# A hybrid decoder layer: v of the first two token tiles from raw x in fp32, and seven of eight products with the norm gain on GpSimd

## The chip, the cores and the metric

The kernel runs on one core of one Trainium2 chip, in one launch. A core has a matrix engine (TensorE, PE in the profile), a vector engine (VectorE, DVE), a scalar engine (ScalarE, ACT), a general engine (GpSimd, POOL) and a sync engine (SyncE, SP) that here only issues DMAs. Each engine takes its instructions in the order of the program, and semaphores order them against each other. SBUF is the on-chip memory of 128 partitions, PSUM the memory that TensorE writes its products to.

The metric is the time of one execution on the device, in microseconds; of several runs the median is given.

## The reference

One layer, 1024 tokens of 1024 channels. Only its head matters here: the RMS norm with its gain, and the projection of the normed input, of which v is 512 columns.

```python
def rms_norm(x, g):
    xf = x.astype(jnp.float32)
    var = jnp.mean(xf * xf, axis=-1, keepdims=True)
    return (xf * lax.rsqrt(var + RMS_EPS) * g.astype(jnp.float32)).astype(x.dtype)

for l in range(DEPTH):                                   # DEPTH = 1
    h = rms_norm(x, norm_mix_pre[l])
    proj = h @ w_in[l]
    q, k, v, cb, cc, cx, g_att, g_conv = jnp.split(proj, IN_SPLITS, axis=-1)
    ...
```

After it come a causal stick-breaking attention over 8 heads of 64, a short gated convolution, their merge with sigmoid gates, an output projection with a norm and a residual, and a feed-forward part with a convolution of its own.

## The kernel before

**Precision.** Most products are made of fp16 halves: an operand is scaled by a power of two and split into a high half (its value in fp16) and a low half (what is left, again in fp16). A product then takes three fp16 passes (`PASSES`: high by high, high by low, low by high). The scale of a weight comes from the sum of its squares: ScalarE squares it with an accumulating output, `total` sums that over the partitions with a tiny matmul against ones and takes a power of two (`pow2_of`). The scale of the normed input, `s_h`, comes from the greatest gain (`g_top`, `g_max`). Where fp32 operands are multiplied without a split, TensorE takes them as fp32.

**Tiles and layouts.** x is cut into eight tiles of 128 tokens, `xt[0]` to `xt[7]`. TensorE needs the normed input with the channels on the partitions. That is `hT`, 128 partitions by 2 halves by 8 blocks of channels by 1024 tokens. A token tile gets there in one of three ways:

- Tile 0: normed in two halves of 512 channels (`norm_halves`, L263), turned by eight TensorE transposes (`turn_halves`, L283) and copied by ScalarE to `h32`, in fp32 (L502). Its v is made by `v_raw` (L353) from `h32` and the raw fp32 `w_v`: eight fp32 products. Its halves of hT are made from `h32` late (L543, L544).
- Tiles 1 and 2: normed, turned by `turn_pe` (L292), and split from PSUM straight into hT (L516, L517 and L526, L527). Their v takes three fp16 passes over eight blocks of channels (`v_pass`, L362).
- Tiles 3 to 7: normed by `norm` (L253), split in SBUF into `x16` (L304 on ScalarE, L305 on VectorE) and turned by two DMA transposes each, issued by SyncE (L308).

**The norm.** The sum of squares is made by ScalarE, or half by ScalarE and half by VectorE in `norm_halves`; GpSimd raises it to the power -1/2 (one number per token); VectorE multiplies x by that number and by the gain in one operation (L259, L275). For tiles 0 and 1 the gain is in PSUM: TensorE spreads the one loaded row of it over 128 partitions by two products with a row of ones (L249). For the others it is `gb`, a tile that a DMA fills with the row repeated.

**v.** `v_end` (L376) takes a tile's v out of PSUM with a scale (L381), makes differences of neighbouring tokens with the help of three small DMAs (L385), and splits them. The scale is 2^-16, or `vs0` for tile 0.

**Order.** SyncE's first loads are written by hand: x0, the first quarter of w_v, x1, the other three quarters, x2, the gain tile `gb`, x3, two tables and x4 to x7. Everything else is put in order by a planner (`Plan`). Each job has an engine, a cost and its reads and writes; `LAND` says when each x tile lands. TensorE jobs keep the order in which they are listed (`seq`), apart from a few, and the planner lists the others by the time at which they can start and by how late they may be. `warm(n)` is n products of a constant tile that nothing reads. After v of tiles 0 to 3 come the first halves of q and k of the first pair of heads (`qk_fill`, L467, products on L459), which read hT of tiles 0 to 3; then v of tile 4 and the second halves of q and k, which read hT of tiles 4 to 7; then the attention units with the other projections between them.

**Buffers.** The slab pool `s` has 12 slots of 4 KB per partition for this part, `wh` has eight buffers for split weights, `pm` three PSUM banks.

Of the kernel before, what the change touches and what calls it, by code (L numbers as in the profile page):

```python
# [18 lines left out]
F32 = mybir.dt.float32  # L19
# [5 lines left out]
P = 128  # L25
# [19 lines left out]
ONE = 2.0 ** 14  # L45


class Layer:
# [84 lines left out]
    def mixer(self, mid):  # L133
        tc, nc, a = self.tc, self.nc, self.a
        hT = self.hp.tile([P, 2, KD, T], F16, tag="hT", name="hT")
        with ExitStack() as ph1:
# [14 lines left out]
            if True:  # L151
# [5 lines left out]
                on1 = self.slot([P, P], F32, "on1")  # L157
# [28 lines left out]
                with tc.manual_schedule(engines={ET.PE, ET.DVE, ET.Activation, ET.SP, ET.Pool}):  # L186
# [28 lines left out]
                    LAND = {0: 4.6, 1: 7.3, 2: 12.9, 3: 15.9, 4: 18.6, 5: 20.0, 6: 21.4, 7: 22.8}  # L215
                    g_row, zero, one_row = given("s", gr, 2.3), given("s", wz), given("s", on1)
                    gbb = given("s", gb, 14.4)
                    xs = {tt: given("s", xt[tt], LAND[tt]) for tt in range(8)}
                    raw_v = [given("ws", st[i], (6.1, 8.7, 10.0, 11.5)[i]) for i in range(4)]
                    sv = given("sm", self.small("sm_v"))  # L220
                    hb = [NOTE() for _ in range(8)]
                    h32 = Buf("s", lambda: self.slot([P, KD, P], F32, "h32"))
# [23 lines left out]
                    gpb = Buf("z", lambda: two_banks("g_ps"))  # L246
                    ps2 = Buf("pm", lambda: pm.tile([P, NH], F32, tag="pm", name="g2"))
                    for c in range(2):
                        M(0.94, lambda c=c: pe.matmul(gpb.t.rearrange("p k t -> p (k t)")[:, ds(c * NH, NH)], on1[0:1, :],  # L249
                                                      gr[0:1, ds(c * NH, NH)], start=True, stop=True), [one_row, g_row], [(gpb, str(c))])  # L250
                    M(0.3, lambda: pe.matmul(ps2.t[:, 0:2], self.ones[0:1, :], g_c.t["g16"][0:1], start=True, stop=True),
                      [g_c], [ps2])
                    def norm(tt):  # L253
                        r, x = Buf("sm", lambda: self.small(f"r_pre{tt}")), xs[tt]
                        A(1.25, lambda: self.sumsq(xt[tt], r.t[:, 0:1], f"n_pre{tt}"), [x], [r])
                        V(0.15, lambda: vec.tensor_scalar(r.t[:, 1:2], r.t[:, 0:1], 1.0 / D, EPS, ALU.mult, ALU.add), [], [r])
                        pl.add("G", 0.6, lambda: pool.tensor_tensor(r.t[:, 2:3], r.t[:, 1:2], self.neghalf, ALU.pow), [], [r])
                        g = gpb if tt < 2 else gbb
                        V(1.28, lambda: vec.scalar_tensor_tensor(  # L259
                            xt[tt], xt[tt], r.t[:, 2:3], g.t.rearrange("p k t -> p (k t)") if tt < 2 else gb,  # L260
                            ALU.mult, ALU.mult), [r, g], [x])

                    def norm_halves(tt, first=(), prior=(), then=None):  # L263
                        r, x = Buf("sm", lambda: self.small(f"r_pre{tt}")), xs[tt]
                        lo, hi = xt[tt][:, :NH], xt[tt][:, NH:]
                        A(0.82, lambda: act.activation(self.junk(f"jk_n_pre{tt}")[:, :NH], lo, AF.Square, accum_out=r.t[:, 0:1]),
                          [(x, "0"), *first], [(r, "0")])
                        V(0.76, lambda: vec.scalar_tensor_tensor(jv.t[:, :NH], hi, 1.0, hi, ALU.mult, ALU.mult,
                                                                 accum_out=r.t[:, 3:4]), [(x, "1"), *prior], [(r, "1"), jv])
                        V(0.15, lambda: vec.tensor_scalar(r.t[:, 4:5], r.t[:, 3:4], 1.0 / D, EPS, ALU.mult, ALU.add), [], [(r, "1")])  # L270
                        V(0.15, lambda: vec.scalar_tensor_tensor(r.t[:, 1:2], r.t[:, 0:1], 1.0 / D, r.t[:, 4:5], ALU.mult, ALU.add),
                          [(r, "0"), (r, "1")], [(r, "2")])
                        pl.add("G", 0.6, lambda: pool.tensor_tensor(r.t[:, 2:3], r.t[:, 1:2], self.neghalf, ALU.pow), [], [(r, "2")])
                        for c, sl in enumerate((slice(0, NH), slice(NH, D))):
                            V(0.66, lambda sl=sl: vec.scalar_tensor_tensor(  # L275
                                xt[tt][:, sl], xt[tt][:, sl], r.t[:, 2:3], gpb.t.rearrange("p k t -> p (k t)")[:, sl],
                                ALU.mult, ALU.mult), [(r, "2"), (gpb, str(c))], [(x, str(c))])
                            if then and c == 0:
                                then(x)
# [3 lines left out]
                    def turn_halves(tt):  # L283
                        pt[tt] = [Buf("pm", lambda: pm.tile([P, KH, P], F32, tag="pm", name=f"pt_pre{tt}a")),
                                  Buf("z", lambda: two_banks(f"pt_pre{tt}b"))]
                        for c in range(2):
                            def f(c=c):
                                for k in range(KH):
                                    pe.transpose(pt[tt][c].t[:, k, :], xt[tt][:, ds((c * KH + k) * P, P)], self.ident)
                            M(0.52, f, [(xs[tt], str(c))], [pt[tt][c]])  # L290
# [11 lines left out]
                    def turn_dma(tt, due=1e9):  # L302
                        b, x = Buf("s", lambda: self.slot([P, 2, D], F16, f"x16_{tt}")), xs[tt]
                        A(1.06, lambda: act.activation(b.t[:, 0, :], xt[tt], AF.Copy, scale=s_h), [x, g_s], [(b, "0")], due=due)  # L304
                        V(1.27, lambda: vec.scalar_tensor_tensor(b.t[:, 1, :], xt[tt], s_h, b.t[:, 0, :], ALU.mult, ALU.subtract),  # L305
                          [x, g_s, (b, "0")], [(b, "1")], due=due)
# [40 lines left out]
                    own = hT[:, :, :, :P]  # L347
# [5 lines left out]
                    def v_raw(*ks):  # L353
                        def f():
                            for k in ks:
                                pe.matmul(pv[0].t, h32.t[:, k, :], st[k // 2][:, ds((k % 2) * NH, NH)], start=k == 0,
                                          stop=k == KD - 1)
                        M(0.87 * len(ks), f, [(h32, str(k // KH)) for k in ks] + [raw_v[k // 2] for k in ks], [pv[0]])
# [13 lines left out]
                    vs0 = Buf("sm", lambda: self.small("vs0"))  # L372

                    vf = {}

                    def v_end(tt):  # L376
                        f = vf[tt] = Buf("s", lambda: self.slot([P, 2, NH], F32, f"vf{tt}"))
                        v, b = v16[tt // 2], vb[tt // 2]
                        pj = lambda e: f.t[:, e].rearrange("p (j two d) -> p j two d", two=2, d=64)
                        sc = lambda: vs0.t[:, 0:1] if tt == 0 else 2.0 ** -16  # L380
                        A(0.58, lambda: act.activation(f.t[:, 0], pv[tt].t, AF.Copy, scale=sc()), [pv[tt]] + ([vs0] if tt == 0 else []),  # L381
# [118 lines left out]
                    square_v(0, 0, slice(0, D), "A")  # L500
                    for c in range(2):
                        A(0.55, lambda c=c: act.activation(h32.t[:, ds(c * KH, KH)], pt[0][c].t[:, :KH], AF.Copy, scale=s_h),  # L502
                          [pt[0][c], g_s], [(h32, str(c))])
                    square_v(1, 1, slice(0, D), "A", [h32])
                    square_v(2, 2, h0, "A")
                    square_v(2, 3, h1, "V", [xs[1]])
                    square_v(3, 4, h0, "A")
                    square_v(3, 5, h1, "V")
                    bv = total("v", sv, lambda: sv.t, 6, True, far=False)
                    V(0.15, lambda: vec.tensor_scalar(vs0.t[:, 0:1], bv.t["s"], 2.0 ** -16, None, ALU.mult), [bv], [vs0])  # L510
                    for k in range(3):
                        v_raw(k)
                    turn_pe(1)
                    for k in range(3, KD):
                        v_raw(k)
                    A(1.1, lambda: act.activation(hT[:, 0, :, ds(P, P)], pt[1].t, AF.Copy, scale=s_h), [pt[1], g_s], [(hb[1], "0")])  # L516
                    V(1.27, lambda: vec.scalar_tensor_tensor(hT[:, 1, :, ds(P, P)], pt[1].t, s_h, hT[:, 0, :, ds(P, P)],  # L517
                                                             ALU.mult, ALU.subtract), [pt[1], g_s, (hb[1], "0")], [(hb[1], "1")])
# [10 lines left out]
                    v_bank(1)  # L529
                    for i in range(4):  # L530
                        v_pass(1, (2 * i, 2 * i + 1), ((0, 0), (1, 0)), first=i == 0)
                    v_bank(2)
                    v_pass(2, range(4), ((0, 0),), first=True)
                    v_pass(2, range(4, 8), ((0, 0),))
                    v_pass(2, range(8), ((1, 0),))
                    for i in range(4):
                        v_pass(1, (2 * i, 2 * i + 1), ((0, 1),), last=i == 3)
# [1468 lines left out]
```

## Time and profile before

| | us |
|---|---|
| three runs: median (lowest to highest) | 1250.1 (1249.38 to 1251.72) |
| the profiled execution, its time on the device | 1250.39 |
| its span, first to last instruction | 1248.7 |

| engine | busy, us | share of the span |
|---|---|---|
| ACT | 856.1 | 69% |
| POOL | 86.3 | 7% |

The other engines' rows stand in the prediction. PE is matrix products; PEld, the loads of the stationary operand, runs beside them. "Busy" for PE contains products whose end is modelled, because they overlap in the array; the step from one start to the next is the better measure of what one costs. A row of the timeline has the start from the beginning of the span, the length, the engine, the line of the kernel, the operation with the tiles that it writes and reads, and in brackets how long the engine was idle before it and what ended that. A row of the waits names who waited, for whom, and the total, the number and the longest of the waits.

### The profile page before, as it was taken

To read this page: it belongs to the slowest core of one execution; us is meant where nothing else is said; L and a number is where in the kernel's file an instruction comes from. 1 tells how busy PE (TensorE), PEld (TensorE's weight loads), DVE (VectorE), ACT (ScalarE), POOL (GpSimd) and SP (SyncE) were. 2 spreads that over 40 slices of the span, in tenths; PEclk is the share of its full clock that TensorE was granted. 3 is DMA by queue.
4 is the path that set the end of the run, shared out by engine and by line. 5 is a ranking of instruction groups with operands and counts; after the bars stand their busy time and mean duration, and the time that the engine had idled before them with its cause. 6 is when DMAs were issued, how large, how long until landed. Compare 5 with 4: busy or idle time off the path is not lost.

```text
span 1248.7 us, 16478 instructions
## 1 busy us (share of the span) xinstructions
PE 1233.2 (99%) x6065; PEld 559.4 (45%) x6065; DVE 1018.6 (82%) x1605; ACT 856.1 (69%) x1247; POOL 86.3 (7%) x113
## 2 busy tenths in 40 slices
PE   9999999999999999999989999999999999999997
PEld 4444444444444444444444444444444444444443
DVE  7888889856998675559899999699589879969866
ACT  7766666736758565755666679778778967878434
POOL 1100000000000000001100001001100300111003
PEclk9999999999999999999999999999999999999999
DMA  8755577660224111656953205415921961594607
GB/s 276 157 128 116 136 129 180 148 150 29 74 74 129 34 65 54 233 189 149 222 144 133 71 23 214 169 34 99 257 82 19 203 184 34 104 251 142 179 1 135
DMA packets 148931, 160.80 MB, mean 129 GB/s; under 512 B 114425, under 2 KB 114553, under 8 KB 148850
## 3 DMA queue, kind: packets, MB, share of 16 engines
q1 hardware_dynamic: 138480, 123.05, 35.3%
q0 software_dynamic: 10368, 36.70, 14.1%
q8 instruction: 47, 0.77, 0.3%
q14 instruction: 34, 0.28, 0.1%
q10 hardware_dynamic: 2, 0.00, 0.0%
HBM read 92.88 MB, written 37.75 MB: 105 GB/s over the span
## 4 chain that ended last, share of the span: by engine, by line
PE 45%; DVE 2%; DMA 2%; issue 1%; ACT 1%; POOL 1%; POOLq 0%; DVEq 0%; SPq 0%; ACTq 0%
PE pq L1601 12%; PE pd L1671 2%; PE pu6b L1425 1%; PE pu10b L1425 1%; PE pu8b L1425 1%; PE pu20b L1425 1%; PE pu19b L1425 1%; PE pu16b L1425 1%; PE pu12b L1425 1%; PE pu4b L1425 1%; PE pu3b L1425 1%; PE pu21b L1425 1%; PE pu18b L1425 1%; PE pu17b L1425 1%; PE pu15b L1425 1%
## 5 line engine op out<-in xcount | busy, mean ns | idle before, releaser
L1425 PEld LDWEIGHTS <-wh_u 128*128 128x128 f16 x1848 | 179.1, 98 | 219.0 <-issue 2.2
L824 ACT ACTIVATE wh_u<-ws_u,sc_u 128x1024 f16<-128x1024 f32 (+1 forms) x66 | 66.5, 1010 | 36.8 <-PE pr_dn L812 7.4
L993 PEld LDWEIGHTS <-wh_g 128*128 128x128 f16 x588 | 57.0, 98 | 68.6
L1605 ACT ACTIVATE st<-pq,sd 128x512 f32<-128x512 f32 x112 | 75.3, 696 | 11.8 <-PE pq L1601 8.6
L1228 PE MATMUL py<-wo,m 128*128 128x512 f16 x384 | 83.3, 379 | 0.0
L826 DVE SCALAR_TENSOR_TENSOR wh_u<-ws_u,sc_u,wh_u 128x1024 f16<-128x1024 f32 (+1 forms) x66 | 72.5, 1104 | 10.4 <-ACT wh_u L824 10.2
L790 POOL DMA_DIRECT2D acc<-st x56 | 43.8, 783 | 426.6 <-ACT st L1605 426.6
L624 DVE TENSOR_TENSOR_SCAN e<-e,mask 128x512 f32<-128x512 f32 (+3 forms) x64 | 48.7, 807 | 13.2 <-ACT e L617 13.2
L1228 PEld LDWEIGHTS <-m 128*128 128x128 f16 x384 | 37.4, 98 | 44.9
L1474 DVE SCALAR_TENSOR_TENSOR ug<-cg,cw_g,ug 128x1023 f32<-128x1023 f32 (+1 forms) x44 | 56.2, 1278 | 1.3 <-ACT ug L1472 1.3
L1474 DVE SCALAR_TENSOR_TENSOR ua<-ca,cw_a,ua 128x1023 f32<-128x1023 f32 (+1 forms) x44 | 56.2, 1278 | 1.1 <-ACT ua L1472 0.9
L617 ACT ACTIVATE e<-z,cz 128x1024 f32<-128x1024 f32 (+3 forms) x48 | 42.3, 896 | 20.4 <-PE z L595 14.8
L66 ACT ACTIVATE jk_u<-ws_u 128x1024 bf16<-128x1024 f32 x44 | 46.5, 1056 | 12.4 <-DMA ws_u<-w_up_nt 12.2
L638 ACT ACTIVATE w<-e 128x1024 f16<-128x1024 f32 (+3 forms) x48 | 38.8, 837 | 12.4 <-DMA wt<-w 6.3
L459 PE MATMUL pcc<-hT,wh_cc 128*128 128x512 f16 x192 | 44.6, 380 | 0.8 <-ACT u L575 0.8
L459 PE MATMUL pk<-hT,wh_k 128*128 128x512 f16 x192 | 43.1, 379 | 0.0
L459 PE MATMUL pq<-hT,wh_q 128*128 128x512 f16 x192 | 43.0, 379 | 0.0
L1601 PE MATMUL pq<-wq,fx 128*128 128x512 f16 x192 | 42.8, 379 | 0.0
L1601 PE MATMUL pq<-wq,fy 128*128 128x512 f16 x192 | 42.7, 379 | 0.0
L923 PE MATMUL pywc<-p,wh_wc 128*128 128x512 f16 x192 | 42.6, 379 | 0.0
L1601 PE MATMUL pq<-wq,fs 128*128 128x512 f16 x192 | 42.2, 379 | 0.0
L624 DVE TENSOR_TENSOR_SCAN e<-e,cr,mask 128x512 f32<-128x512 f32 x32 | 39.8, 1273 | 1.2 <-ACT e L617 1.0
(796 smaller groups left out, 2731.1 us busy)
## 6 DMA issues: line engine op xcount, KB each, us to landing
acc<-st POOLq DMA_DIRECT2D x56, 512.0 KB, 5.9
ws_u<-w_up_nt SPq DMA_DIRECT2D x44, 512.0 KB, 4.1
ds<-w_down SPq DMA_DIRECT2D x18, 512.0 KB, 14.8
wt_g<-w_in_nt SPq DMA_DIRECT2D x14, 512.0 KB, 3.5
x<-x SPq DMA_DIRECT2D x8, 512.0 KB, 8.6
wr_wo<-w_out SPq DMA_DIRECT2D x8, 512.0 KB, 3.6
ws_wo<-w_out SPq DMA_DIRECT2D x8, 512.0 KB, 4.3
xr<-x SPq DMA_DIRECT2D x8, 512.0 KB, 4.3
```

The source lines that it names most:

```text
L66: self.nc.scalar.activation(self.junk(f"jk_{name}"), src, AF.Square, accum_out=acc)
L459: pe.matmul(ps.t, w.t[:, wi, ds(k * P, P)], hT[:, hi, k, ds(c * NH, NH)], start=k == 0 and p == 0, stop=k == KD - 1 and p == 2)
L624: vec.tensor_tensor_scan(x, x, m[:, ::-1], ONE if diag else cr.t[:, h:h + 1], ALU.mult, ALU.max)
L790: j = pl.add(eng, 0.45 if eng == "SP" else 1.14, lambda: e.dma_start(dst(), srcf(), **kw), r, [b] if w is None else w, ahead=AHEAD["load"] ...
L824: A(C["As" if big else "Ash"], lambda: act.activation(dst.t[:, 0, dsl], src.t[:, ssl], AF.Copy, scale=sb.t["s"]), [(src, sreg), sb], [(dst ...
L826: V(C["V" if big else "Vh"], lambda: vec.scalar_tensor_tensor(dst.t[:, 1, dsl], src.t[:, ssl], sb.t["s"], dst.t[:, 0, dsl], ALU.mult, ALU. ...
L993: pe.matmul(b.t, p.w[wt].t[:, wi, ds(wc * NH + k * P, P)], block(i, h, k), start=first and n == 0, stop=n == 3 * KH - 1, skip_group_check= ...
L1228: pe.matmul(b.t, m16[k].t[:, h_, ds(tt * P, P)], wo[k].t[:, w_, sl], start=k == 0 and p == 0, stop=k == 7 and p == 2)
L1425: pe.matmul(b.t, p.w[wt].t[:, wi, ds(wc * NH + k * P, P)], block(i, h, k), start=first and n == 0, stop=n == 3 * KH - 1, skip_group_check= ...
L1474: V(C["V"], lambda lag=lag: vec.scalar_tensor_tensor(u.t[:, lag:], c.t[:, :T - lag], sm.t[:, 2 - lag:3 - lag], u.t[:, lag:], ALU.mult, ALU ...
L1601: pe.matmul(b.t, fa[p].t[:, h, ds(fo * NH + tt * P, P)], wa[p].t[:, x, ds(wo * NH, NH)], start=first and n == 0, stop=n == 5, skip_group_c ...
L1605: A(C["Ah"], lambda tt=tt, b=b, st=st: act.activation(st.t[:, tt % 2, :], b.t, AF.Copy, scale=q.sd.t[:, 0:1]), [b, q.sd], [(st, str(tt % 2 ...
```

## The change

- x of tiles 0 and 1 is turned before it is normed: `turn_raw` transposes the raw tile on TensorE, and VectorE copies it out of PSUM and multiplies it by the gain there, where the channels lie on the partitions and the gain is one number for each partition and block (`gt`). The result is `h32[0]` and `h32[1]`, now in the pool `wh`.
- For `gt` the row of the gain is turned into eight columns by eight fp32 products with a single one (`g_turn`). The spread of the gain into PSUM is gone. `on1` is a small tile.
- v of both tiles is made by `v_raw` in fp32 from raw w_v. The norm's factor is applied to v when ScalarE takes it out of PSUM (`vs[tt]`).
- hT of both tiles is made later: they go through `norm` and `turn_dma`, as tiles 3 to 7 do.
- For the tiles in `GAINED`, all but tile 2, `norm` is a product with the gain tile on GpSimd, and the norm's factor times `s_h` is the scale with which `turn_dma` splits.
- All four squares of w_v are on ScalarE, over whole tiles. Six of eleven warm-up products are left.
- SyncE loads all of w_v ahead of x1, and `LAND` is changed to go with it.

```diff
+GAINED = (0,1,3,4,5,6,7,)
...
-                    if i == 0:
-                        load_x(1)
+                load_x(1)
...
-                    gpb = Buf("z", lambda: two_banks("g_ps"))
-                    for c in range(2):
-                        M(0.94, lambda c=c: pe.matmul(gpb.t.rearrange("p k t -> p (k t)")[:, ds(c * NH, NH)], on1[0:1, :],
-                                                      gr[0:1, ds(c * NH, NH)], start=True, stop=True), [one_row, g_row], [(gpb, str(c))])
+                    def g_turn():
+                        for k in range(KD):
+                            pe.matmul(ps2.t[:, ds(8 + k, 1)], gr[0:1, ds(k * P, P)], on1[0:1, 0:1], start=True, stop=True,
+                                      skip_group_check=True)
+                    M(0.9, g_turn, [g_row], [(ps2, "t")])
+                    V(0.15, lambda: vec.tensor_copy(gt.t[:, 0:KD], ps2.t[:, ds(8, KD)]), [(ps2, "t")], [gt])
...
+                        if tt in GAINED:
+                            V(0.12, lambda: self.mul(r.t[:, 3:4], r.t[:, 2:3], s_h), [g_s], [r])
+                            pl.add("G", 2.4, lambda: pool.tensor_tensor(xt[tt], xt[tt], gb, ALU.mult), [gbb], [x])
+                        else:
+                            V(1.28, lambda: vec.scalar_tensor_tensor(xt[tt], xt[tt], r.t[:, 2:3], gb, ALU.mult, ALU.mult), [r, gbb], [x])
...
+                    def turn_raw(tt):
...
+                            M(0.9, f, [xs[tt]], [pt[tt][c]])
+                            V(0.72, lambda c=c: vec.tensor_tensor(
+                                h32[tt].t[:, ds(c * KH, KH)], pt[tt][c].t[:, :KH],
+                                gt.t[:, ds(c * KH, KH)].rearrange("p (k o) -> p k o", o=1).broadcast_to([P, KH, P]), ALU.mult),
+                              [pt[tt][c], gt], [(h32[tt], str(c))])
...
+                        sc, dep = ((lambda: rs[tt].t[:, 3:4]), rs[tt]) if tt in GAINED else ((lambda: s_h), g_s)
...
+                        if tt < 2:
+                            V(0.12, lambda: self.mul(vs[tt].t[:, 0:1], vs0.t[:, 0:1], rs[tt].t[:, 2:3]), [vs0, rs[tt]], [vs[tt]])
...
-                    warm(4)
-                    norm_halves(0, then=lambda x: V(0.15, lambda: vec.tensor_copy(gs[:, 3:5], ps2.t[:, 0:2]), [ps2, (x, "0")], [g_s]))
-                    turn_halves(0)
-                    warm(2)
-                    norm_halves(1, (), ())
...
+                    turn_raw(0)
+                    warm(1)
                     v_bank(0)
...
+                    stats(0)
+                    for i in range(4):
+                        square_v(i, i, slice(0, D), "A")
+                    bv = total("v", sv, lambda: sv.t, 4, True, far=False)
+                    V(0.15, lambda: vec.tensor_scalar(vs0.t[:, 0:1], bv.t["s"], s_h, 2.0 ** -16, ALU.mult, ALU.mult), [bv, g_s], [vs0])
+                    for k in range(KD - 1):
+                        v_raw(0, k)
+                    stats(1)
+                    turn_raw(1)
+                    v_raw(0, KD - 1)
+                    v_bank(1)
+                    for k in range(KD):
+                        v_raw(1, k)
...
-                    A(1.0, lambda: act.activation(own[:, 0], h32.t, AF.Copy), [h32], [(hb[0], "0")], ahead=OWN)
-                    V(1.15, lambda: vec.tensor_tensor(own[:, 1], h32.t, own[:, 0], ALU.subtract), [h32, (hb[0], "0")], [(hb[0], "1")], ahead=OWN)
...
                     v_end(2)
+                    for tt in range(2):
+                        norm(tt)
+                        turn_dma(tt)
                     qk_fill(0, "q", (0,))
```

More of the change, by code (lines that the diff above doesn't have):

```diff
@@ L257, in norm @@
                         pl.add("G", 0.6, lambda: pool.tensor_tensor(r.t[:, 2:3], r.t[:, 1:2], self.neghalf, ALU.pow), [], [r])
[L258 to L279, printed above, removed]
@@ L372, in mixer @@
                     vs0 = Buf("sm", lambda: self.small("vs0"))
+                    vs = {tt: Buf("sm", lambda tt=tt: self.small(f"vs{tt}")) for tt in range(2)}
                     vf = {}
@@ L504, in mixer @@
[L504 to L512, printed above, removed]
```

64 lines of the change are left out of this document (26 added, 38 removed).

## The prediction

> **What bounds the kernel now.** I read the page first, then TensorE's waits in the first 70 us, then the timeline of the stretch that is edited, then the windows of VectorE and GpSimd beside it.
>
> ```profile
> span 1248.7 us, 16478 instructions
> PE 1233.2 (99%) x6065; PEld 559.4 (45%) x6065; DVE 1018.6 (82%) x1605; ACT 856.1 (69%) x1247; POOL 86.3 (7%) x113
> ```
>
> TensorE leaves 15.5 us of the span empty. What is saved or lost on it early is therefore passed on to the end nearly one for one, as long as no later wait eats it. Its waits before 70 us:
>
> ```profile
> PE warm L242 <- DVE wz L156: 1.7, 1, 1.7
> PE pv L367 <- DVE hT L527: 0.3, 1, 0.3
> ```
>
> So from 3.92 us on TensorE is fully occupied, but not by useful work: gain broadcasts and warm-up products fill it until x is normed. The columns below are start, length, engine.
>
> ```profile
> 3.92 3.78 PE L249 MATMUL g_ps<-g_row,on 1*128 1x512 f32 x4
> 7.63 1.89 PE L242 MATMUL warm<-wz 128*128 128x512 f16 x4
> 9.32 1.06 PE L289 MATMUL pt_pre0a<-ident,x 128*128 128x128 f32 x4
> 10.17 1.06 PE L289 MATMUL pt_pre0b<-ident,x 128*128 128x128 f32 x4
> 11.02 1.06 PE L242 MATMUL warm<-wz 128*128 128x512 f16 x2
> 11.88 3.27 PE L356 MATMUL pv<-ws_v,h 128*128 128x512 f32 x6
> ...
> 15.86 1.02 PE L356 MATMUL pv<-ws_v,h 128*128 128x512 f32 x2
> 16.72 0.17 PE L343 MATMUL pr_v<-rb_v,ones 128*128 128x1 bf16 x1
> 16.75 3.68 PE L356 MATMUL pv<-ws_v,h 128*128 128x512 f32 x8
> ...
> 31.98 5.34 PE L367 MATMUL pv<-wh_v,hT 128*128 128x512 f16 x24
> 37.16 5.34 PE L459 MATMUL pq<-hT,wh_q 128*128 128x512 f16 x24
> ...
> 54.58 1.47 PE L459 MATMUL pq<-hT,wh_q 128*128 128x512 f16 x6
> ```
>
> The first product of v starts at 11.88, the first of q at 37.16. Those 25.28 us are v of tiles 0 to 3. The question is when the q product starts afterwards, and whether its hT, and the hT of tiles 4 to 7 for the row at 54.58, is there.
>
> **The clock in the first 12 us.** The window view grants 1.00 everywhere, yet the records show two rates:
>
> ```profile
> 12.73 0.30 PEld L356 LDWEIGHTS pv<-ws_v,h 128*128 128x128 f32 x1 [0.52 <-issue]
> 13.27 0.19 PEld L356 LDWEIGHTS pv<-ws_v,h 128*128 128x128 f32 x1 [0.24 <-issue]
> 13.70 0.19 PEld L356 LDWEIGHTS pv<-ws_v,h 128*128 128x128 f32 x1 [0.24 <-issue]
> ```
>
> A half product of v takes 0.85 (11.88 to 12.73) and later 0.43 (13.27 to 13.70). Two warm products take 0.86 (11.02 to 11.88), 0.43 each, while 24 later ones of the same shape take 5.18 (31.98 to 37.16), 0.216 each. So TensorE runs at half rate until about 12.73. That is 5.1 us after it began unbroken work on all 128 rows (7.63). The gain broadcast before it, on one row, seems not to have counted.
>
> **The change, part by part.**
>
> *Start of v.* Two rows say when data is there:
>
> ```profile
> 4.36 0.63 ACT L266 ACTIVATE jk_n_pre<-x 128x512 bf16<-128x512 f32 x1 [1.72 <-DMA x<-x]
> 5.70 1.06 ACT L314 ACTIVATE jk_v<-ws_v 128x1024 bf16<-128x1024 f32 x1 [0.62 <-DMA ws_v<-w_v]
> ```
>
> x0 has landed at 4.36 and the first w_v at 5.70. Removed ahead of the first product are the broadcast (3.92 to 7.50), four warm products (1.69) and the norm. In their place stands the gain turned to columns: eight products of one column. A full fp32 product shows as two records (L249: two products, x4), so this is 16 weight loads. No row shows it. From below it costs 16 times 0.03 (the step from pr_v at 16.72 to 16.75), 0.5 us. From above, 16 times 0.21, a half-rate transpose with its fp32 load (four in 0.85, 9.32 to 10.17), 3.4 us. I take 3.4, because each one has a 128-column fp32 load like the transpose. Then the transposes start at 7.32, take 1.70 (9.32 to 11.02), one warm product 0.43: v starts at **9.45**, 2.43 earlier. VectorE copies the first half of the transposes meanwhile (one PSUM pass, 0.69 by L476 below, from 8.17 to about 9.1).
>
> *Half rate.* Counting 5.1 us from 7.32, the full rate comes at 12.42. The work now done at half rate lasts 12.42 - 9.45 = 2.97 instead of 0.85, and half of that is lost.
>
> *Tile 1 in fp32.* Eight products of two records of 0.43, 6.93 us, replace 24 fp16 products, 5.18: **+1.75**.
>
> *Sum on TensorE.* Work between first v and first q at full rate, before: 25.28 less 0.43 (half of 0.85), less 0.11 (the 0.54 record from 12.73 to 13.27), less 0.26 of wait, is 24.48. After: 24.48 + 1.75 + 0.11 = 26.34. Start of q = 26.34 + (9.45 + 12.42)/2 = 37.28, against 37.16: **+0.1**. With the turn at 0.5 us the transposes begin at 4.42, v at 6.55, full rate at 9.52: 34.4, **-2.8**. If transposes don't count towards the full rate, it comes 5.1 after 9.02: 38.1, **+1.0**.
>
> *VectorE and GpSimd.* From the gain's broadcast tile on (about the eighth load of 1.34, 4.36 to 5.70, so near 14) until 50 us:
>
> ```profile
> 14.40:50.00 35.60, 35.34 (x163) 16.58 (x162) 32.13 (x56) 30.33 (x44) 6.87 (x6) 1.00 0.76 197
> ```
> ```profile
> L259 DVE SCALAR_TENSOR_TENSOR x<-x,r_pre,g_pre 128x1024 f32<-128x1024 f32 x6 | 7.6, 1280 | 0.4 <-POOL r_pre L257 0.4
> L305 DVE SCALAR_TENSOR_TENSOR x<-x,g_pre,x 128x1024 f16<-128x1024 f32 x5 | 6.3, 1278 | 0.0
> ...
> L527 DVE SCALAR_TENSOR_TENSOR hT<-pt_pre,g_pre,hT 128x1024 f16<-128x1024 f32 x1 | 1.3, 1277 | 0.0
> L517 DVE SCALAR_TENSOR_TENSOR hT<-pt_pre,g_pre,hT 128x1024 f16<-128x1024 f32 x1 | 1.3, 1272 | 0.0
> L544 DVE TENSOR_TENSOR hT<-h,hT 128x1024 f16<-128x1024 f32 x1 | 1.2, 1214 | 0.0
> L256 DVE TENSOR_SCALAR r_pre<-r_pre 128x1 f32<-128x1 f32 x6 | 0.9, 150 | 1.5 <-ACT jk_n_pre L66 1.5
> L476 DVE SCALAR_TENSOR_TENSOR q<-pq,q 128x512 f16<-128x512 f32 x1 | 0.7, 692 | 0.0
> ```
>
> VectorE is busy 32.1 of 35.6 us. It loses five of the six L259 (6.4), L517 and L544 (2.5). It gains two more low halves like L305 (2.6), two copies of tile 1's transposes (1.4) and seven small products (1.05). Net -3.9, so 7.4 us idle.
>
> GpSimd gets seven products of 128x1024. No row has one. From below it is 1.28, VectorE's L259; from above 2.35, eight times its own 0.294 for 128 columns:
>
> ```profile
> 1.67 0.29 POOL masks.py:199 TENSOR_SCALAR_AFFINE_SELECT ident<-ident 128x128 f32<-128x128 f32 x1
> 15.95 0.55 POOL L257 TENSOR_TENSOR r_pre<-r_pre,neghalf 128x1 f32<-128x1 f32 x1 [4.96 <-DVE r_pre L256]
> 22.49 1.27 DVE L522 SCALAR_TENSOR_TENSOR wh_v<-ws_v,s0v,wh_v 128x1024 f16<-128x1024 f32 x1
> 22.65 1.52 POOL L257 TENSOR_TENSOR r_pre<-r_pre,neghalf 128x1 f32<-128x1 f32 x1 [6.15 <-DVE r_pre L256]
> 31.47 1.28 DVE L259 SCALAR_TENSOR_TENSOR x<-x,r_pre,g_pre 128x1024 f32<-128x1024 f32 x1
> 31.69 1.47 POOL L257 TENSOR_TENSOR r_pre<-r_pre,neghalf 128x1 f32<-128x1 f32 x1 [0.35 <-DVE r_pre L256]
> ```
>
> I take 2.35: 16.5 us in all (9.0 from below). The rows show more: GpSimd's tiny pow takes 0.55 alone, but next to a VectorE operation with two SBUF operands it ends 0.41 after that operation's end both times (24.17 against 23.76, 33.16 against 32.75). The two exclude each other, at least with VectorE first. Whether a product of 2.35 us then holds VectorE up as long, no row shows: from below 0.
>
> [...]
>
> *What hides it.* The last low halves and their transposes, which the q product of 54.58 needs:
>
> ```profile
> 46.85 2.48 DVE L305 SCALAR_TENSOR_TENSOR x<-x,g_pre,x 128x1024 f16<-128x1024 f32 x2
> 43.74 7.28 SPq L308 DMA_TRANSPOSE hT<-x  x5
> DMA to landing us min/median/max: 3.1/3.3/4.5
> ```
>
> VectorE ends them at 49.33; the last transpose starts at 49.7 and lands 3.3 later, at 53.0: **1.6 us of slack**. If all GpSimd time excludes VectorE, 16.5 - 7.4 = 9.1 us come on top. But GpSimd can run beside operations that read PSUM or are tiny: L527 (1.3), tile 1's copies (1.4), two L476 (1.4), some 25 small ones of 0.15 (3.8), 7.9 in all. So hT is late by 1.2 to 9.1 us; I take 1.2, inside the slack, because the products of tiles 0 and 1 can run early, while VectorE still has gaps. The wait is then nothing.
>
> *The transposes.* Tiles 0 and 1 now reach hT by four more DMA transposes on SP, 7.28/5 = 1.46 each, 5.8 us, behind their two new norms and ahead of the q product. Behind them in SP's queue are the moves of v and the weight loads. Their inputs need only the gain tile, so they can start in the twenties, where SP has waits; I cost them at nothing. If that cover is gone, the q product at 37 waits for the last of them.
>
> **The forecast.** The profiled execution took 1250.39 us, its span 1248.7; the median shown is 1250.1, 0.3 lower. 1250.39 + 0.1 + 0 = 1250.5; I say **1250.6**: no change, within what a measurement of this kernel can tell (0.2%, 2.5 us). Chance 0.50, own range 1248 to 1252.5.
>
> **Rivals.**
>
> *The turn of the gain is short.* Then v starts near 6.55 and the full rate comes near 9.5: 1250.39 - 2.8 = 1247.6, with less if q's hT isn't early enough. For it: 0.03 for a tiny product; against it: each has its own fp32 load. The fast end lies just past the bound, so faster has 0.17.
>
> *GpSimd's products hold VectorE up (slower).* Place: VectorE between 14 and 50 us, where hT of tiles 4 to 7 is made. Price: midway between 1.2 and 9.1 is 5.1 late, less 1.6 of slack: +3.5, or 1254; at the end +7.5, 1257.9. It decides from about 4 us of lateness, where the wait at the second half of q passes 2.5. For it: the pow rows, and 90% busy VectorE. Against it: freed time. Chance 0.28.
>
> *The q product waits for tiles 0 and 1.* ScalarE is 30.3 of 35.6 us busy and has to make their high halves in time; two transposes late (2 x 1.46) is +2.9, 1253.3. Chance 0.05.
>
> Faster 0.17, same 0.50, slower 0.33. The range reaches from 1247.4, the fast rival, to 1256, most of the lock's.
>
> **What would show it.** First v record near 9.5 and the turn as 16 loads of some 0.2: the TensorE sum. Half-product records changing from 0.85 to 0.43 near 12.4. GpSimd products of about 2.35, and VectorE gaps released by nothing it waits for, or longer operations, beside them: the lock. TensorE's idle time before the q rows near 37 and 54 gives the stalls; none of them means that hT is in time. I am wrong if the turn takes under 1.5 us, if the full rate comes elsewhere, or if TensorE waits for hT by more than 2 us.

## The result, and the profile after

| | us |
|---|---|
| before: median of five runs (lowest to highest) | 1250.1 (1248.83 to 1252.8) |
| after: median of five runs (lowest to highest) | 1260.93 (1259.57 to 1262.09) |
| ratio of after to before, 95% interval | 1.0083 (1.0071 to 1.0095) |
| profiled execution after, and its span | 1260.93, 1259.2 |

The kernel became 10.8 us slower, past the upper end of the predicted range (1256). Spans say the same: 1259.2 against 1248.7, 10.5 more. The page of the changed kernel:

```profile
span 1259.2 us, 16485 instructions
PE 1234.3 (98%) x6064; PEld 561.6 (45%) x6064; DVE 1025.0 (81%) x1600; ACT 857.2 (68%) x1245; POOL 104.6 (8%) x120
```

TensorE is busy 1.1 us longer than before, but empty for 24.9 us instead of 15.5. So nearly all of the loss is waiting. TensorE's waits in the first 80 us (who waits, for whom, total, number, longest):

```profile
PE pr_k L344 <- DVE rb_k L339: 3.6, 1, 3.6
PE pt_pre L297 <- DVE x L275: 3.3, 1, 3.3
PE warm L242 <- DVE on L159: 1.7, 1, 1.7
PE z L583 <- DVE k L479: 1.5, 1, 1.5
PE g L255 <- DVE g L234: 0.9, 1, 0.9
```

All of them name VectorE. The two largest are new: the transposes of tile 2 wait for its norm (L275), and the sum behind the scale of k's weight waits for a one-column cast. The timeline of TensorE shows where they lie:

```profile
3.92 3.57 PE L251 MATMUL g<-on,g_row 1*128 1x1 f32 x16
...
10.68 6.06 PE L356 MATMUL pv<-ws_v,h 128*128 128x512 f32 x12
16.58 0.17 PE L344 MATMUL pr_v<-rb_v,ones 128*128 128x1 bf16 x1
...
24.44 1.09 PE L297 MATMUL pt_pre<-ident,x 128*128 128x128 f32 x8 [3.28 <-DVE x L275]
25.37 7.01 PE L356 MATMUL pv<-ws_v,h 128*128 128x512 f32 x12
...
41.21 0.16 PE L344 MATMUL pr_k<-rb_k,ones 128*128 128x1 bf16 x1 [3.62 <-DVE rb_k L339]
41.23 5.34 PE L367 MATMUL pv<-wh_v,hT 128*128 128x512 f16 x24
46.41 5.34 PE L462 MATMUL pq<-hT,wh_q 128*128 128x512 f16 x24
```

The first q product starts at 46.41 instead of 37.16, 9.25 us late. That delay adds up: v starts 1.20 earlier (10.68 for 11.88); the two waits cost 3.28 + 3.62; the twelve fp32 products from 25.37 take 6.85 up to the next row instead of twelve times 0.43, 1.69 more; tile 1 in fp32 is taken at the predicted 1.75 (sixteen records of 0.43 for twenty-four of 0.216). Together 9.14. Behind q, the first scores (z) wait 1.53 for k on VectorE, as the list of waits shows; that makes 10.8, and the span ends 10.5 late.

So VectorE is late. The window from 14.4 to 50 us, which the prediction read for the kernel before, and the stretch of the slow fp32 products (columns: window, length, then busy time and number of instructions of PE, PEld, DVE, ACT and POOL, then the granted clock):

```profile
14.40:50.00 35.60, 28.70 (x110) 13.23 (x109) 32.17 (x44) 22.19 (x30) 24.21 (x12) 0.95 0.64 172
25.80:29.40 3.60, 3.60 (x6) 1.53 (x5) 3.60 (x3) 2.50 (x3) 3.60 (x2) 0.53 0.56 165
```

VectorE is busy as long as before (32.17 against 32.13 us), but gets through 44 instructions instead of 56. They have become longer. Its timeline, with GpSimd's below it:

```profile
16.81 0.16 DVE L72 TENSOR_SCALAR s0v<-pr_v 128x1 int32<-128x1 int32 x1 [5.37 <-PE pr_v L344]
...
18.79 2.22 DVE L79 TENSOR_TENSOR r_pre<-r_pre,g_pre 128x1 f32<-128x1 f32 x1
20.94 0.68 DVE L287 TENSOR_TENSOR h<-pt_pre1b,g_t 128x512 f32<-128x512 f32 x1
21.54 2.85 DVE L275 SCALAR_TENSOR_TENSOR x<-x,r_pre,g_pre 128x1024 f32<-128x1024 f32 x1
24.31 1.27 DVE L516 SCALAR_TENSOR_TENSOR wh_v<-ws_v,s0v,wh_v 128x1024 f16<-128x1024 f32 x1
...
38.79 2.29 DVE L79 TENSOR_TENSOR r_pre<-r_pre,g_pre 128x1 f32<-128x1 f32 x1
41.01 0.14 DVE L339 CAST rb_k<-sm_k 128x1 bf16<-128x1 f32 x1
```
```profile
17.36 0.55 POOL L265 TENSOR_TENSOR r_pre<-r_pre,neghalf 128x1 f32<-128x1 f32 x1 [6.33 <-DVE r_pre L264]
...
18.65 4.66 POOL L273 TENSOR_TENSOR x<-x,g_pre 128x1024 f32<-128x1024 f32 x2
...
38.73 2.34 POOL L273 TENSOR_TENSOR x<-x,g_pre 128x1024 f32<-128x1024 f32 x1
```

Read them side by side. One product on GpSimd takes 2.34 us (38.73 to 41.07). The product of two columns of one number each on VectorE (L79), 0.15 us otherwise, begins at 38.79 and ends at 41.08. The same pair stands at 18.65 and 18.79. Then L275, which takes 1.27 to 1.28 us where nothing holds it, starts at 21.54 during GpSimd's second product and ends 1.08 after that one (23.31). L287, one of whose operands is in PSUM, keeps its 0.68, although the second product runs at that time. GpSimd in its turn is held: its seven products take 20.8 us, not 7 x 2.34. The groups of the small product and of GpSimd's product over the whole stage (busy, mean in ns, idle before and what ended it):

```profile
L79 DVE TENSOR_TENSOR r_pre<-r_pre,g_pre 128x1 f32<-128x1 f32 x7 | 9.5, 1362 | 0.1
L273 POOL TENSOR_TENSOR x<-x,g_pre 128x1024 f32<-128x1024 f32 x7 | 20.8, 2983 | 4.9 <-ACT jk_n_pre L67 4.9
```

The last two rows of VectorE's timeline show how this reaches TensorE: the cast that pr_k waits for takes 0.14, but stands behind the held product.

### The profile page after: what moved, and what is told of

Its sections match the earlier page's. It is cut to its first block, busy times and chain, and to the rows that moved or that the text cites. A ratio compares the mean times of both kernels' runs of the same rounds, so it can differ in the third digit from the quotient of the medians.

```text
span 1259.2 us, 16485 instructions
## 1 busy us (share of the span) xinstructions
PE 1234.3 (98%) x6064; PEld 561.6 (45%) x6064; DVE 1025.0 (81%) x1600; ACT 857.2 (68%) x1245; POOL 104.6 (8%) x120
## 4 chain that ended last, share of the span: by engine, by line
PE 45%; DVE 3%; DMA 1%; ACT 1%; issue 1%; POOL 1%; POOLq 0%; DVEq 0%; ACTq 0%
PE pq L1589 12%; PE pd L1659 2%; PE pu6b L1413 1%; PE pu10b L1413 1%; PE pu8b L1413 1%; PE pu20b L1413 1%; PE pu19b L1413 1%; PE pu16b L1413 1%; PE pu12b L1413 1%; PE pu4b L1413 1%; PE pu3b L1413 1%; PE pu21b L1413 1%; PE pu18b L1413 1%; PE pu17b L1413 1%; PE pu15b L1413 1%
```

## The experiments

Each kernel ran against the kernel before on the same chip, and its ratio is to that. Three theories stood against each other: that GpSimd's products **hold** VectorE's operations with two SBUF operands; that the **planner** puts VectorE's work in a bad order, because it takes the turn of the gain for 0.9 us where it takes 3.57; and that GpSimd is merely slow and hands x **on late**.

**The same order with short products.** GpSimd multiplies 128 of the 1024 channels; the others are left without the gain. The order on all engines stays.

```diff
-pl.add("G", 2.4, lambda: pool.tensor_tensor(xt[tt], xt[tt], gb, ALU.mult), [gbb], [x])
+pl.add("G", 2.4, lambda: pool.tensor_tensor(xt[tt][:, :P], xt[tt][:, :P], gb[:, :P], ALU.mult), [gbb], [x])
```

> The changed kernel with one edit: GpSimd multiplies only the first 128 of the 1024 channels by the gain, the other 896 are left without it; the order of the instructions on all engines stays as it is. Theory A (GpSimd's products hold VectorE's operations with two SBUF operands for their whole 2.34 us, and TensorE waits for those): the products shrink to 0.6 us or less, TensorE's waits of 3.3 us (tile 2's transposes), 3.6 us (the sum for k's scale) and 1.5 us (the first attention scores) and the half-rate stretch after 25 us go, time 1250 to 1253 us. Rival B (the new order itself is late: two more tiles through DMA transposes, fp32 v of tile 1, TensorE's place for tile 2's transposes): no change, 1259 to 1262 us.

1252.15 us, ratio to before 1.0011 (1.0001 to 1.0020). Nearly the whole loss is gone. The group of small products, and the first q product:

```profile
L79 DVE TENSOR_TENSOR r_pre<-r_pre,g_pre 128x1 f32<-128x1 f32 x7 | 1.4, 214 | 0.1
```
```profile
38.97 5.34 PE L462 MATMUL pq<-hT,wh_q 128*128 128x512 f16 x24
```

The seven small products take 1.4 us instead of the 9.5 in the changed kernel. The order made with the wrong cost is still there, so by itself it costs 1.5 us at most (1252.15 against 1250.65 for the kernel before on this chip). But a short product also hands x on early, so the third theory is not excluded.

**GpSimd busy as long, but reading a quarter.** Two products of 128 channels, and between them two memsets of a tile that nothing reads. The other 768 channels are left without the gain.

```diff
+rs, mjunk = {}, att.tile([P, 720], F32, tag="mjunk", name="mjunk", bufs=1)
-pl.add("G", 2.4, lambda: pool.tensor_tensor(xt[tt], xt[tt], gb, ALU.mult), [gbb], [x])
+pl.add("G", 2.4, lambda: (pool.tensor_tensor(xt[tt][:, :P], xt[tt][:, :P], gb[:, :P], ALU.mult),
+    pool.memset(mjunk, 0.0), pool.memset(mjunk, 0.0),
+    pool.tensor_tensor(xt[tt][:, P:2 * P], xt[tt][:, P:2 * P], gb[:, P:2 * P], ALU.mult)), [gbb], [x])
```

> The changed kernel with GpSimd's product of 1024 channels replaced by a product of channels 0 to 127, two memsets of an unread tile of 720 columns, and a product of channels 128 to 255; channels 256 to 1023 are left without the gain. GpSimd is busy for each tile about as long as in the changed kernel (estimate 2.2 to 2.6 us) and hands x on as late, but for most of that time it reads nothing. The order on the other engines stays. Theory A (it is GpSimd's reading that holds VectorE): near the run with the short products (1252.2), 1251 to 1254 us, and no operation of VectorE over 1.5 us in place of its 0.15 or 1.28. Rival D (what is late is x itself, which is handed on 2.34 us after the product starts): near the changed kernel, 1258 to 1261 us.

1250.85 us, ratio 1.0008 (0.9999 to 1.0017). The windows view, GpSimd's timeline, and the group of small products:

```profile
14.40:50.00 35.60, 34.11 (x144) 15.89 (x143) 28.88 (x59) 27.50 (x37) 27.18 (x35) 1.00 0.80 195
```
```profile
18.19 0.46 POOL L273 TENSOR_TENSOR x<-x,g_pre 128x128 f32<-128x128 f32 x1
18.59 1.45 POOL L273 MEMSET mjunk<- 128x720 f32 x2
20.00 2.16 POOL L273 TENSOR_TENSOR x<-x,g_pre 128x128 f32<-128x128 f32 x2
22.11 1.45 POOL L273 MEMSET mjunk<- 128x720 f32 x2
23.52 1.24 POOL L273 TENSOR_TENSOR x<-x,g_pre 128x128 f32<-128x128 f32 x1
```
```profile
L79 DVE TENSOR_TENSOR r_pre<-r_pre,g_pre 128x1 f32<-128x1 f32 x7 | 1.8, 255 | 2.6 <-POOL r_pre L265 2.6
```

GpSimd is busy 27.18 us in this window, more than in the changed kernel (24.21), and hands tile 1 on at 24.76, later than there (18.65 + 4.66 = 23.31). VectorE gets 59 instructions done in 28.88 us. So neither the time on GpSimd nor the late x costs the 10 us. What is left is what a memset does not do: read its operands from SBUF over all 1024 channels. L275, which lies beside memsets for most of its time (from 19.18; they last from 18.59 to 20.04), takes 1.27 us, against 2.85 in the changed kernel.

**The small product with one SBUF tensor.** The norm's factor comes as a per-partition scalar instead of a second tensor.

```diff
-V(0.12, lambda: self.mul(r.t[:, 3:4], r.t[:, 2:3], s_h), [g_s], [r])
+V(0.12, lambda: vec.tensor_scalar(r.t[:, 3:4], r.t[:, 2:3], s_h, None, ALU.mult), [g_s], [r])
```

> The changed kernel with one edit: the product of two 128x1 columns ahead of each GpSimd product (rstd times the gain's scale) is a tensor_scalar with a pointer to the second column, instead of a tensor_tensor of two SBUF columns; the order stays. Theory A: four of these seven took 2.2 to 2.3 us beside a GpSimd product instead of 0.15; if it is the second SBUF operand that is held, they take 0.15 to 0.2 now, but the next operation with two large operands is held in their place for what is left of the product, so 1 to 5 us of the 10.8 come back: 1256 to 1260 us. If a column read by pointer is held too: 1260 to 1262 us and the 2.2 us stay.

1257.62 us, ratio 1.0053 (1.0036 to 1.0070). The group in this run, and TensorE's largest wait:

```profile
L272 DVE TENSOR_SCALAR r_pre<-r_pre,g_pre 128x1 f32<-128x1 f32 x7 | 1.3, 203 | 0.1
```
```profile
PE pr_q L344 <- DVE r_pre L264: 3.9, 1, 3.9
```

In this form the operation is not held (0.20 each). A third of the loss goes, inside the range that was expected. What is left of the hold falls on the large operations that have two SBUF operands by their nature (L275 still takes 2.63), and the wait moves to q's scale.

**Four pieces.** Each product in four of 256 columns, so that VectorE can get in between.

```diff
+pl.add("G", 2.4, lambda: [pool.tensor_tensor(xt[tt][:, ds(256 * i, 256)], xt[tt][:, ds(256 * i, 256)],
+    gb[:, ds(256 * i, 256)], ALU.mult) for i in range(4)], [gbb], [x])
```

> The changed kernel with each GpSimd product cut into four of 256 channels, one behind the other; the same work, order kept on all engines. [...] If VectorE has to wait for the whole chain of pieces: 1259 to 1262 us.

By theory A a held operation waits for one piece only, an estimated 0.6 us (a quarter of 2.34): 0.5 to 0.8 us for a small product and 1253 to 1257 us in all were expected of it.

1258.19 us, ratio 1.0069 (1.0056 to 1.0083), between the two ranges. GpSimd's first two tiles and all its products of the stage, and VectorE afterwards:

```profile
19.07 9.49 POOL L273 TENSOR_TENSOR x<-x,g_pre 128x256 f32<-128x256 f32 x8
L273 POOL TENSOR_TENSOR x<-x,g_pre 128x256 f32<-128x256 f32 x28 | 30.8, 1132 | 1.5 <-ACT jk_n_pre L67 1.5
```
```profile
29.11 0.67 DVE L79 TENSOR_TENSOR r_pre<-r_pre,g_pre 128x1 f32<-128x1 f32 x1 [2.49 <-POOL r_pre L265]
```

A small product on VectorE now takes 0.67, as expected. But GpSimd is held for longer: the seven tiles take it 30.8 us instead of 20.8, and four pieces that met only small operations of VectorE took 2.77 (at 38.96). Its next norm factor comes late, and VectorE waits for that (2.49). The sharing has been turned round, not removed. Both edits together:

```diff
-V(0.12, lambda: self.mul(r.t[:, 3:4], r.t[:, 2:3], s_h), [g_s], [r])
+V(0.12, lambda: vec.tensor_scalar(r.t[:, 3:4], r.t[:, 2:3], s_h, None, ALU.mult), [g_s], [r])
...
+pl.add("G", 2.4, lambda: [pool.tensor_tensor(xt[tt][:, ds(256 * i, 256)], xt[tt][:, ds(256 * i, 256)],
+    gb[:, ds(256 * i, 256)], ALU.mult) for i in range(4)], [gbb], [x])
```

> The split products and the pointer form of the 128x1 products together. Theory A: the small ones aren't held at all, the large ones wait 0.6 us or less each: 1251 to 1255 us. If the two gains don't add (the pointer form only moves the wait to the next large operation): the time of the split alone.

1257.80 us, ratio 1.0068 (1.0055 to 1.0082). The gains do not add: not the time of theory A, but that of the split alone, the other reading.

**Only the products, in the kernel before.** The kernel before with the products of tiles 3 to 7 on GpSimd and the norm's factor in the split, in the form of the change. v of tiles 0 and 1 stays as it was; the planner orders anew.

```diff
-V(1.28, lambda: vec.scalar_tensor_tensor(
-    xt[tt], xt[tt], r.t[:, 2:3], g.t.rearrange("p k t -> p (k t)") if tt < 2 else gb,
-    ALU.mult, ALU.mult), [r, g], [x])
+if tt > 2:
+    rs[tt] = r
+    V(0.12, lambda: self.mul(r.t[:, 3:4], r.t[:, 2:3], s_h), [g_s], [r])
+    pl.add("G", 2.4, lambda: pool.tensor_tensor(xt[tt], xt[tt], gb, ALU.mult), [gbb], [x])
+else:
+    V(1.28, lambda: vec.scalar_tensor_tensor(xt[tt], xt[tt], r.t[:, 2:3], gb, ALU.mult, ALU.mult), [r, g], [x])
...
+r = rs[tt]
-A(1.06, lambda: act.activation(b.t[:, 0, :], xt[tt], AF.Copy, scale=s_h), [x, g_s], [(b, "0")], due=due)
+A(1.06, lambda: act.activation(b.t[:, 0, :], xt[tt], AF.Copy, scale=r.t[:, 3:4]), [x, r], [(b, "0")], due=due)
```

> The kernel before with only the other half of the change: the products with the gain of tiles 3 to 7 (five, not seven) on GpSimd as the change does them, all of tiles 0 to 2 as before. Theory A: each holds VectorE for up to 2.3 us in place of 1.28 us of its own work, and the planner does not know it: slower by 2 to 6 us, 1252 to 1256 us. If GpSimd's products harm only together with the new start: within 1.5 us of before.

1253.15 us, ratio 1.0026 (1.0016 to 1.0036), as theory A expected. TensorE now waits 1.84 for VectorE in v (for 0.26 before) and 1.80 for k ahead of the scores. VectorE shows the same signature without the rest of the change:

```profile
32.99 2.30 DVE L78 TENSOR_TENSOR r_pre<-r_pre,g_pre 128x1 f32<-128x1 f32 x1 [0.58 <-POOL r_pre L259]
39.59 3.38 DVE L311 SCALAR_TENSOR_TENSOR x<-x,r_pre,x 128x1024 f16<-128x1024 f32 x1
```

**TensorE kept busy ahead of tile 2's transposes.** After the wait of 3.28 the granted clock is 0.53 for a while (the window from 25.8 above). 32 products that nothing reads go ahead of these transposes, in the order as it is.

```diff
-for k in range(KD):
-    pe.transpose(pt[tt].t[:, k, :], xt[tt][:, ds(k * P, P)], self.ident)
+for k in range(32 + KD):
+    pe.transpose(pt[tt].t[:, k - 32, :], xt[tt][:, ds((k - 32) * P, P)], self.ident) if k >= 32 else pe.matmul(pt[tt].t[:, k % KD, :], self.ones, self.ones, start=True, stop=True)
```

> The changed kernel with 32 products of a constant tile, which nothing reads, on TensorE ahead of tile 2's transposes, where it idles 3.3 us; the order of all else stays. Theory A has the idle time cost a second time, because the fp32 products of v after it run at half rate (five records of 0.85 us instead of 0.43, 2.1 us): with the idle time filled they stay at 0.43, and the time falls by 1 to 2.1 us to 1259 to 1260 us. If the half rate has nothing to do with the idle time, or the v products aren't on the path: 1260 to 1262 us, 0.85 us records after 25 us as before.

1260.83 us, ratio 1.0078 (1.0063 to 1.0094): nothing gained, against what was expected. TensorE's timeline in this run:

```profile
10.68 7.02 PE L356 MATMUL pv<-ws_v,h 128*128 128x512 f32 x12
...
26.35 5.32 PE L356 MATMUL pv<-ws_v,h 128*128 128x512 f32 x12
...
42.19 0.16 PE L344 MATMUL pr_k<-rb_k,ones 128*128 128x1 bf16 x1 [4.12 <-DVE rb_k L339]
42.21 8.30 PE L367 MATMUL pv<-wh_v,hT 128*128 128x512 f16 x24
50.35 5.34 PE L462 MATMUL pq<-hT,wh_q 128*128 128x512 f16 x24
```

The products from 26.35 do run at the full rate, but what they save is waited for at pr_k (4.12 for 3.62), and now the pass behind that wait is slow (8.30 for 5.34). In this profile the first twelve products are slow for longer, too (7.02 for 6.06). The run is therefore inconclusive on what the 1.69 is worth. It shows something else: its q product starts 3.94 later than in the changed kernel, and its span, 1260.0, is only 0.8 longer. The wait of 1.53 ahead of the first scores is not there any more, and the second q pass starts 2.09 later (68.18 for 66.09). So lateness at the first q is not passed on whole; where the rest of it went was not followed.

**No product on GpSimd.** VectorE makes them all, and the planner orders anew.

```diff
-GAINED = (0,1,3,4,5,6,7,)
+GAINED = ()
```

> The changed kernel with GAINED empty: all eight products with the gain on VectorE, together with rstd in one operation of 1.28 us, as tiles 2 to 7 had it before; the rest of the change stays, the planner orders it anew. Theory A: VectorE gets 7 x 1.28 us of work more and loses the 16.4 us in which GpSimd excluded it; no wait of TensorE over 1 us before the first q, time 1249 to 1253 us. Rival B: still 1256 us or more.

1262.05 us, ratio 1.0089 (1.0074 to 1.0104): a clear miss for theory A, and in the range of rival B. TensorE's two largest waits:

```profile
PE pq L462 <- DMA hT<-x: 2.7, 1, 2.7
PE px0c L981 <- ACT cax L1016: 2.6, 1, 2.6
```

So this form of the change, in this order, has costs of its own. Only part of them lies in the stretch that was edited: the third q pass starts at 95.14 against 87.84 in the kernel before, 7.3 late, but the span (1260.1) ends 11.4 late. The second wait above lies near 317 us, and the kernel before does not have it.

**The planner told the truth.** The turn of the gain is entered with 4.6 us; once with the change as it is, once without products on GpSimd.

```diff
-M(0.9, g_turn, [g_row], [(ps2, "t")])
+M(4.6, g_turn, [g_row], [(ps2, "t")])
```

> The changed kernel with one number changed: the planner reckons 4.6 us for the turn of the gain instead of 0.9 (3.57 us and the 0.91 us of wait behind it in the trace). It orders all engines anew, nothing is computed otherwise. Theory C (a good part of the loss is an order made for a TensorE that is 4 us ahead of the real one: the small product for w_v's scale stands behind six products of v, and VectorE idles 5.4 us for it): 1254 to 1258 us, that idle time under 3 us. Theory A alone: GpSimd still holds VectorE for the same 16 us: 1259 to 1262 us.

1268.81 us, ratio 1.0153 (1.0138 to 1.0168), above both ranges. v starts at 9.63, and VectorE's wait for pr_v falls from 5.37 to 2.27, as meant. The work that comes earlier then runs into GpSimd's products: two operations of VectorE that take 1.27 alone, L516 and L275, take 3.40 and 3.36. Even so the first q starts at 45.15, earlier than in the changed kernel (46.41), and the third q pass at 96.92 against 98.94. What makes this kernel 7.9 us slower than the changed one comes later, among it two waits of TensorE near 155 to 240 us and near 323 us:

```profile
PE o L583 <- DMA wt<-w: 4.9, 3, 3.3
PE px0c L981 <- ACT cax L1016: 2.6, 1, 2.6
```

In the changed kernel the first of them is 0.5, and the second is missing. A new order at the head changes later stages as well, so this run says little about theory C.

> Both: GAINED empty (all eight products with the gain on VectorE) and 4.6 us for the turn of the gain in the planner. Theories A and C together: 1249 to 1254 us. If moving v of two tiles to raw x costs by itself, through four more DMA transposes and VectorE's work for them: 1256 us or more, with TensorE waiting for hT ahead of the first q products, as the run with GAINED empty did (2.7 us).

1255.22 us, ratio 1.0041 (1.0026 to 1.0056). Without GpSimd the true cost is worth 6.3 us (11.4 above the kernel before on its chip, now 5.1). The largest wait that is left is in the first q product, for hT of tiles 0 and 1 (v has read that of tiles 2 and 3 before):

```profile
37.85 0.38 PE L462 MATMUL pq<-hT,wh_q 128*128 128x512 f16 x1
41.25 5.14 PE L462 MATMUL pq<-hT,wh_q 128*128 128x512 f16 x23 [3.03 <-DMA hT<-x]
```

**These halves due earlier**, on top of that:

```diff
-turn_dma(tt)
+turn_dma(tt, -6.0)
```

> The run with all products on VectorE and the true cost of the turn (1255.2), with the halves of tiles 0 and 1 given a due time 6 us before v's own, so that the planner puts them earlier on VectorE. That run waited 3.0 us for hT ahead of the first q products. If that wait was their late place in VectorE's order: it goes below 1 us and the time falls to 1250 to 1253 us. If VectorE's total work is the cause, another wait takes its place: 1254 us or more.

1258.04 us, ratio 1.0066 (1.0053 to 1.0080). The wait for hT goes, and another takes its place, which was the second reading:

```profile
PE pq L462 <- DVE wh_q L449: 1.7, 1, 1.7
```

But this wait does not make the time. The third q pass starts at 90.60, 2.8 later than in the kernel before, and the span (1256.4) ends 7.7 later; the rest is lost in later stages. In none of the three orders that were tried did VectorE make all the products and the late hT without a loss. No version ran faster than the kernel before.

## Why the prediction was wrong

**Right.** Two costs that no row had shown were sized well: the turn of the gain takes 3.57 us for 16 records (3.4 predicted), and one product on GpSimd 2.34 (2.35). VectorE's freed time is there when nothing holds it: 28.88 us busy in the window with the memsets, where 32.1 less 3.9 was forecast. By the sum of the result, without the waits and their slow products q would start at 46.41 - 3.28 - 3.62 - 1.69 = 37.82, against 37.28 predicted. Of the 0.54 between, most is a wait that I missed: behind the turn, the small product L255 waits 0.91 for VectorE, so v starts at 10.68, not 9.45, half of which counts. Where the hold is all but gone and the order kept, the time is 0.7 us (memsets, 1250.85 against 1250.11) and 1.5 us (short products) above the kernel before. So "no change" is about what the change is worth without the hold, as far as kernels that leave out most of the gain can say.

**Right by luck.** The full rate was forecast for 12.42, from 5.1 us of unbroken work. The loads of v's half products show it at about 12.29:

```profile
11.53 0.34 PEld L356 LDWEIGHTS pv<-ws_v,h 128*128 128x128 f32 x1 [0.52 <-issue]
12.29 0.19 PEld L356 LDWEIGHTS pv<-ws_v,h 128*128 128x128 f32 x1 [0.42 <-issue]
12.72 0.19 PEld L356 LDWEIGHTS pv<-ws_v,h 128*128 128x128 f32 x1 [0.24 <-issue]
```

But the work on 128 rows began at 8.50, not 7.32, so it took 3.8 us, not 5.1; a late start and a short half rate made up for each other. Whether the products on one row (3.92 to 7.49) count, which the forecast left out, no run shows. Nor is it one number: from 10.68 to pr_v, TensorE's same list took 5.43 in the run with the pointer, 5.90 in the changed kernel and 6.85 in the one with 32 more products.

**The step that failed** is "GpSimd can run beside operations that read PSUM or are tiny", with its "7.9 in all" and "I take 1.2, inside the slack". By it the wait of TensorE was nothing. In its place TensorE waited 3.28 and 3.62 us for VectorE before the first q and 1.53 behind it, and lost 1.69 on slow products. The step failed twice:

- Tiny is not safe. I counted some 25 small operations (3.8 us) as room for GpSimd. But what decides is the operands: a product of 128x1 by 128x1, both in SBUF, takes up to 2.32 us instead of 0.15, and holds everything behind it on VectorE. Operations with an operand in PSUM did run beside GpSimd, as I had said (L287 0.68), and so did the small product with a scalar operand (0.20).
- "The products of tiles 0 and 1 can run early, while VectorE still has gaps" did not come true. VectorE idles 5.37 us until 16.81, because pr_v stands behind six fp32 products of v in TensorE's order; GpSimd's norm factors need VectorE's results from behind that wait, and so GpSimd sits idle as well (6.33), with the products behind it in its order. The gap and the products never meet. So they meet VectorE's work: four of the seven small products (together 9.5 us for what takes 7 x 0.15), L275 (+1.57) and low halves of later tiles are held.

**The rival was right in kind, not in place or price.** "GpSimd's products hold VectorE up" had a chance of 0.28 and 1254 to 1257.9. I looked for the harm at the second half of q, with 1.6 us of slack to eat up. It came earlier, where VectorE feeds TensorE with no slack: at tile 2's norm (3.28) and at the scale of k (3.62). A range built from lateness at one deadline left out the deadlines before it. None of the three signs under "I am wrong if" showed: the third asks for waits for hT, and TensorE waited for a normed tile and a cast. Longer operations on VectorE beside GpSimd's products, the sign named for the lock, did show.

**The rival on tiles 0 and 1** (chance 0.05, 1253.3) did not come true in the changed kernel, nor in the two runs in its order where the hold is all but gone: none of them waits for hT at the first q. It shows only where VectorE makes all the products and the order is new: 2.70 and 3.03 us.

**Open.** The kernel without products on GpSimd is slower than before by 5 to 11 us, depending on the planner's costs and due times. How much of that is VectorE's added work, and how much merely another order of later stages, was not told apart. For the same reason it stays open what the planner's wrong cost of the turn is worth in the changed kernel; the run with short products bounds it only where the hold is gone.

## What to carry to other kernels

A product given to GpSimd was not taken off VectorE here where VectorE worked with two SBUF operands meanwhile: count up to nearly its whole length as VectorE's time (up to 2.17 of 2.34 us here), and look first at small VectorE operations that feed another engine, since a held 0.15 us operation holds all that stand behind it (here a cast of 0.14 us that TensorE waited 3.62 us for). Where such work must lie beside GpSimd, give it a scalar or a PSUM operand instead of a second SBUF tensor (0.20 and 0.68 us here, not held); by itself the scalar brought back a third here, because larger operations were held next. To find out whether an engine is slow or is holding another, keep the order and the length and change only what the suspect reads. A run in which a planner orders anew compares more than the edit: here it moved several us in stages hundreds of us later.

## What the runs showed of the hardware that was not expected

- The hold does not scale with the size of the held operation: a 128x1 operation of 0.15 us lasts up to 2.32, a 128x1024 operation of 1.27 us up to 3.40, so both are held up to some 2.1 to 2.2 us. The same arithmetic on 128x1 with a scalar operand takes 0.20.
- Quarter products cost more beside VectorE than whole ones: 30.8 us for seven tiles against 20.8.
- The granted clock drops to 0.53 after a wait of 3.28 us at 24.44, but the pass after the longer wait of 3.62 at 41.21 takes its full-rate 5.18. Without products on GpSimd, the 23 products behind a wait of 2.70 take 6.66 up to the next row, those behind a wait of 3.03 in the run with the true cost 4.98. And up to 10.68 the changed kernel and the one with 32 more products run the same program, yet the next twelve products take 6.06 in one profile and 7.02 in the other. The length of a wait alone does not decide. What else does, no run here shows.
